# Fixed places for the modulation-weight halves among the product steps, and the gate input's load behind the solve's

## The chip, the cores and the metric

The kernel runs on one core of a Trainium2 chip. The metric is the device time of one execution in microseconds (us), the median of several runs. The engines are PE (TensorE, the matrix multiplier), DVE (VectorE), ACT (ScalarE), POOL (GpSimd) and SP (SyncE, which here issues nearly all DMA transfers). Each engine works through its own instruction list in order and waits for the others by semaphores.

## The reference

The kernel computes one decoder block on x of 512 positions by 1024 columns, all in float32, with a conditioning vector c:

```
mod = silu(c) @ w_ada + b_ada                  # 6 x 1024 numbers
shift1, scale1, gate1, shift2, scale2, gate2 = split(mod, 6)
h = rms_norm(x, norm1_w) * (1 + scale1) + shift1
p = h @ w_in                                   # 47 column tiles of 128
y_a = gated_deltanet(...)                      # recurrence over 8 chunks, gated by silu(z)
y_b = rwkv7_time_mix(...)                      # recurrence over 8 chunks
merged = sigmoid(gl_a) * (y_a @ w_branch_gdn) + sigmoid(gl_b) * (y_b @ w_branch_rwkv)
x = x + gate1 * (merged @ w_out)
h = rms_norm(x, norm2_w) * (1 + scale2) + shift2
x = x + gate2 * conv_glu(h, w_ffn_in, conv_ffn, w_ffn_out)
return rms_norm(x, norm_f_w)
```

What matters here is `mod`: its parts 1 and 2 are needed at the very start, gate1 at the product with w_out, shift2 and scale2 at the second norm (ahead of the first product of the channel mixer), and gate2 at the end.

## The kernel before

Everything is held transposed: 128 columns on the partitions, 512 positions along the row. A weight tile is 128 x 1024. Each weight and each input is split in a high and a low part of type fp32r (`whi`, `wlo`; `hh`, `hl`), and `mm3` makes three matmuls of one product step (lines 186, 189 and 190): high by high, high by low, low by high. A product of eight steps is 24 matmuls. The split of a weight tile is a cast on ACT (`whi<-raw`, L145) and a subtraction on DVE (`wlo<-raw,whi`, L148); there are two buffers each of `raw`, `whi` and `wlo`.

The large products wait in a list, `queue`, and `stream` hands them out step by step. `fill(n)` puts n steps between the instructions of the small, latency-bound stages, `need` goes on until a product is done, and `drain` empties the list. The order of the program is: input norm and the first seven tiles of w_in; the preparation of the gated delta rule with a triangular solve; its recurrence (8 chunks); the preparation of the second solve, `rsolve` (L843 to L849); the gate stage, in which the gated delta output is multiplied with silu(z) and becomes the input of the eight branch products `bg`; the second recurrence (RWKV-7, 8 chunks); the eight branch products `br`, the two last gate tiles among them (`last_gate`); the eight products `o` with w_out, each with its residual on DVE (L1027); the second norm (L307 to L309); the 44 products `fi` and the eight products `fo` of the channel mixer. The products T_RK, T_RR, T_RV, T_Z, T_GA and T_GB are tiles of w_in, in this order from tile 15 to 46.

The modulation weights are worked on DVE, not PE: one column tile j of `mod` is a product and sum along the row of a 128 x 1024 piece of w_ada with `cond`. Tiles 0 to 15 are done ahead of the first product. The other 32 are cut in two halves each, 64 in all, kept in `ada_rest` in order of j. `ada_half` loads one half (256 KB) on SP into the tile `wada`, of which there is one buffer, and reduces it on DVE (L209) with a second short instruction that reads the accumulator. The second half of a tile starts from the sum of the first. `A2` (L1057) is (1 + scale2) * norm2_w for the second norm and needs tiles 32 to 39, that is the first 48 halves of `ada_rest`.

A scheduler takes the program as written and orders each engine's list by data, buffers and its own costs; `tc.add_manual_dep` with `after` adds a constraint on this order only, without a wait on the chip. In the kernel before, `stream` calls `ada_half` for `late` halves when it takes up a product (3 for each T_GA, 4 for six T_GB, 2 for each o), with no constraint except that the first reduce stands behind one instruction of the preparation (`last["gate"]`).

In the gate stage each of four `zt` tiles is loaded from `zsc` (L871), put through Silu on ACT, and multiplied on DVE (L873); `zt` has the two buffers of the tag `sg`. The second solve starts by loading `lt` from `lsc_r` (L563), and DVE scales it (L564).

Of the kernel before, what the change touches and what calls it, by code (L numbers as in the profile page):

```python
# [18 lines left out]
ALU = mybir.AluOpType  # L19
# [4 lines left out]
T = 512  # L24
KT = 8
# [30 lines left out]
def body(ctx, tc, io, out, tap=lambda name, ap: None):  # L56
# [20 lines left out]
    mm = lambda: bank("mm", 2)  # L77
# [97 lines left out]
        pe.matmul(p, ones_r, lo, start=False, stop=True)  # L175


    last = {"step": None, "hold": False, "gate": None, "norm": None}

    def step(*a, **k):  # L180
        last["step"] = pe.matmul(*a, **k)  # L181
# [1 line left out]
    def mm3(p, w, j, x, start, stop):  # L183
        hi, lo = (a[j] for a in w)
        xh, xl = x
        i = pe.matmul(p, hi, xh, start=start, stop=False)  # L186
        if last["hold"]:
            tc.add_manual_dep(i.ins, last["step"].ins.name, after, reason="place")
        pe.matmul(p, hi, xl, start=False, stop=False)  # L189
        pe.matmul(p, lo, xh, start=False, stop=stop)  # L190
        return i


# [8 lines left out]
        if last["norm"] is not None:  # L202
            tc.add_manual_dep(i.ins, last["norm"].ins.name, after, reason="place")

    def ada_half(j, u):
        w = wp.tile([128, T], F32, name="wada", tag="wada")
        part = slice(T * u, T * u + T)
        sp.dma_start(w, io["w_ada"][j][:, part])
        i = dve.tensor_tensor_reduce(out=w, in0=w, in1=cond[:, part], scale=1.0,  # L209
                                 scalar=half[:, j:j + 1] if u else col("b_ada", j), op0=ALU.mult, op1=ALU.add,  # L210
                                 accum_out=(mod if u else half)[:, j:j + 1])
        if last["gate"] is not None:
            tc.add_manual_dep(i.ins, last["gate"].ins.name, after, reason="place")
            last["gate"] = None

    first_half = []
    ada_rest = [(j, u) for j in range(16, 48) for u in range(2)]


# [10 lines left out]
    def stream():  # L230
        while queue:
            it = queue.pop(0)
            for nx in [it] + queue[:it["ahead"]]:
                if nx["begin"] is not None:
                    nx["begin"]()
                    nx["begin"] = None
            for _ in range(min(it["late"], len(ada_rest))):
                ada_half(*ada_rest.pop(0))
            for i, q in enumerate(it["pieces"]):
                for a in (it["pieces"][i:] + [b for nx in queue[:2] for b in nx["pieces"]])[:2]:  # L240
                    if a["w"] is None:
                        a["w"] = weights(a["src"], a["n"] * 128, a["spare"])
                if it["halves"]:
                    continue
                if i == 0:
                    p = it["psum"]()
                for k in range(q["n"]):
                    at = q["k0"] + k
                    mm3(p, q["w"], k, it["xs"][at], at == 0, at == it["n"] - 1)
                    if at == it["n"] - 1:  # L250
                        it["evac"](p)
                        done.add(it["label"])
                    yield
            for u in range(2 if it["halves"] else 0):
                part = slice(H * u, H * u + H)
                p = it["psum"]()[:, 0:H]
                for q in it["pieces"]:
                    for k in range(q["n"]):
                        at = q["k0"] + k
                        mm3(p, q["w"], k, [x[:, part] for x in it["xs"][at]], at == 0, at == it["n"] - 1)  # L260
                        yield
                it["evac"](p, u, part)
                done.add(it["label"])
# [120 lines left out]
    sp.dma_start(cons, io["cons"])  # L384

    def inproj(t, evac, psum=mm, begin=None):
        queue.append(product(t, io["w_in"][t], hx, evac, psum, late=4 if t >= T_GB else 3 if t >= T_GA else 0, begin=begin))


    omu = const.tile([128, 15], F32, name="omu")  # L390
# [93 lines left out]
    dve.tensor_tensor(s3, s3, s1, op=ALU.mult)  # L484
    dve.scalar_tensor_tensor(s3, sx, 0.0, s3, op0=ALU.max, op1=ALU.add)
    fn(nea, col("a_log", 0, 4), AF.Exp)
    last["gate"] = dve.scalar_tensor_tensor(gl, s3, -1.0, bc(nea), op0=ALU.mult, op1=ALU.mult)


    def l2norm(dst, scale):  # L490
# [62 lines left out]
    def solve(sv, name, work):  # L553


        lsc = dr.tile([128, 32, 32], F32, name=f"lsc_{name}")
        tsc = dr.tile([128, 32, 32], F32, name=f"tsc_{name}")
        usc = dr.tile([128, 32, 32], F32, name=f"usc_{name}")
        for e, b, i0, rows in quads():
            sp.dma_start(lsc[i0:i0 + 32].rearrange("i s t -> s i t"), sv[rows, :, 32 * b:32 * b + 32])  # L560
        wk = slot(work).rearrange("p (a t s) -> p a t s", a=2, t=32)
        lt, ti = wk[:, 0], wk[:, 1]
        sp.dma_start(lt, lsc)  # L563
        dve.tensor_scalar(ti, lt.rearrange("p s t -> p t s"), -1.0, None, op0=ALU.mult)  # L564
        pool.affine_select(out=ti, in_=ti, pattern=[[1, 32], [-1, 32]], base=0, channel_multiplier=0,
                           compare_op=ALU.is_gt, fill=0.0)
        pr = tp.tile([128, 1024], F32, name="pr", tag="pr")
        for j in range(1, 31):
            n = 31 - j
            q = pr[:, :n * j].rearrange("p (t c) -> p t c", c=j)  # L570
            dve.tensor_tensor(q, lt[:, j, j + 1:32].unsqueeze(2).broadcast_to([128, n, j]),
                              ti[:, j, 0:j].unsqueeze(1).broadcast_to([128, n, j]), op=ALU.mult)
            dve.tensor_tensor(ti[:, j + 1:32, 0:j], ti[:, j + 1:32, 0:j], q, op=ALU.subtract)
        dve.memset(ti.rearrange("p t s -> p (t s)")[:, ::33], 1.0)
        sp.dma_start(tsc, ti)
        tt = pr.rearrange("p (s t) -> p s t", s=32)
        act.copy(tt, ti.rearrange("p t s -> p s t"))
        sp.dma_start(usc, tt)
        t1 = lt
        for e, b, i0, rows in quads():  # L580
            if b == 1:
                pool.memset(sv[rows, :, 0:32], 0.0)
            sp.dma_start(sv[rows, :, 32 * b:32 * b + 32], usc[i0:i0 + 32].rearrange("i s t -> s i t"))
            if b == 0:
                sp.dma_start(t1[rows], tsc[i0:i0 + 32].rearrange("i t s -> t i s"))
        yield
        for h in range(2):
            i_ = slice(16 * h, 16 * h + 16)
            p = pa().rearrange("p (i t) -> p i t", i=16)
            ht = tmp("sg").rearrange("p (i t) -> p i t", i=16)  # L590
            for i in range(16):
                for e in range(2):
                    lo_r, hi_r = slice(64 * e, 64 * e + 32), slice(64 * e + 32, 64 * e + 64)
                    pe.matmul(p[hi_r, i, :], sv[lo_r, 16 * h + i, 32:64], t1[lo_r, 16 * h + i, :],
                              start=True, stop=True)
            fill(2)
            for e in range(2):
                hi_r = slice(64 * e + 32, 64 * e + 64)
                act.copy(ht[hi_r], p[hi_r])
            p = pa().rearrange("p (i t) -> p i t", i=16)  # L600
            for i in range(16):
                for e in range(2):
                    lo_r, hi_r = slice(64 * e, 64 * e + 32), slice(64 * e + 32, 64 * e + 64)
                    pe.matmul(p[lo_r, i, :], ht[hi_r, i, :], sv[hi_r, 16 * h + i, 32:64],
                              start=True, stop=True)
            fill(2)
            for e in range(2):
                lo_r = slice(64 * e, 64 * e + 32)
                act.mul(sv[lo_r, i_, 32:64], p[lo_r], -1.0)
# [258 lines left out]
    ga_l = [tmp_r(tag) for tag in ("acc", "acc", "sq", "sq")]  # L868
    for ct in range(4):
        zt, sg = tmp("sg"), tmp("rs")  # L870
        sp.dma_start(zt, zsc[ct])  # L871
        fn(zt, zt, AF.Silu)
        dve.tensor_tensor(sg, go[:, ct], zt, op=ALU.mult)  # L873
        split(ga_h[ct], ga_l[ct], sg)
# [137 lines left out]
    for n in range(KT):  # L1012
        if n in (0, 3):
            g = KT - 2 + n // 3
            queue.append(product(T_GB + g, io["w_in"][T_GB + g], hx, last_gate(g), ahead=1))
        queue.append(product(("br", n), io["w_br"][n], bx, merge(n), begin=merge_in(n), ahead=1))
    x2s = [slot(9), slot(3)]
    x2 = lambda k: x2s[k // 4][:, T * (k % 4):T * (k % 4) + T]
    for n in range(KT):
# [29 lines left out]
        rstd_of(p, 1.0 / D, rstd2[:, part])  # L1049

    for n in range(KT):
        queue.append(product(("o", n), io["w_out"][n], mx, residual(n, x2, 16, keep, total2), late=2, halves=n == KT - 1))
    need(("o", KT - 2))
    table(EXP)
    while ada_rest:
        ada_half(*ada_rest.pop(0))
    dve.scalar_tensor_tensor(A2, mod[:, 32:40], 1.0, col("norm2", 0, 8), op0=ALU.add, op1=ALU.mult)  # L1057
    rstd2 = tmp("rs")
    drain()
# [43 lines left out]
        return f  # L1103

    for i in range(7, 2 * NF):
        queue.append(product(("fi", i), io["w_fi"][i], h2, (glu_up if i % 2 else glu_gate)(i // 2)))
    prefetch()
    for i in range(7):
        (glu_up if i % 2 else glu_gate)(i // 2)(ffn_ps[i])
# [114 lines left out]
```

## Time and profile before

| what | value |
| --- | --- |
| median of 3 runs | 935.42 us (933.39 to 936.28) |
| the profiled execution | 937.31 us, span 935.6 us |
| PE busy | 876.3 us (94%) |
| DVE busy | 533.3 us (57%) |
| ACT busy | 419.2 us (45%) |
| halves of the modulation weights | 64 loads from 47.2 to 476.5 us of the span, 2.7 us from issue to landing (median) |

The span is the time from the first to the last instruction that the profiler saw. Busy time is the sum over an engine's instructions. In the rows that follow, "L186 PE MATMUL ps_mm<-hh,whi" is an instruction of line 186 on PE that writes `ps_mm` and reads `hh` and `whi`; "[4.70 <-ACT tmp_sp L94]" says that the engine was idle for 4.70 us before it and that an instruction of line 94 on ACT, which writes `tmp_sp`, ended that wait. PEld is PE's loading of weights, which overlaps its matmuls. PEclk is the granted clock of PE as a share of full speed.

### The profile page before, as it was taken

The numbers are of one execution on the slowest core, as the hardware profiler recorded it, in microseconds if no ns is written. First come the engines' busy times: TensorE is split into PE (matmuls) and PEld (weight loads), VectorE is DVE, ScalarE is ACT, GpSimd is POOL, SyncE is SP. The second block draws the span as 40 slices with busy tenths as digits, with TensorE's granted clock in tenths as the row PEclk, the third lists the DMA queues.
The fourth block names the chain that finished last, engine by engine and source line by source line (L and its number), as shares of the span: only waits on it lengthen the run. The fifth ranks groups of instructions, "written<-read, shape, count | busy, mean of one in ns | idle before, by whom it ended". The sixth has DMA issues, their size and how long they took to land.

```text
span 935.6 us, 13853 instructions
## 1 busy us (share of the span) xinstructions
PE 876.3 (94%) x5459; PEld 687.7 (74%) x5459; DVE 533.3 (57%) x858; ACT 419.2 (45%) x680; POOL 95.2 (10%) x91
## 2 busy tenths in 40 slices
PE   2999999999989978899999999999999999999996
PEld 1886577677656666677668888888888888888885
DVE  5987859824696786255476537564445445332233
ACT  5367543734554747632465335343333333333231
POOL 1000300000352300001230120000000000010112
PEclk9999999997999989899999999999999999999998
DMA  9841245363323367644546542322322322533322
GB/s 332 283 149 67 91 105 185 109 166 112 103 82 113 69 213 267 162 147 148 183 158 202 171 141 84 111 91 92 109 92 90 105 99 90 179 98 100 107 80 91
DMA packets 81119, 125.72 MB, mean 134 GB/s; under 512 B 26045, under 2 KB 42813, under 8 KB 80990
## 3 DMA queue, kind: packets, MB, share of 16 engines
q1 hardware_dynamic: 81054, 124.83, 42.2%
q8 instruction: 43, 0.70, 0.3%
q14 instruction: 22, 0.18, 0.1%
HBM read 110.13 MB, written 14.16 MB: 133 GB/s over the span
## 4 chain that ended last, share of the span: by engine, by line
PE 69%; DVE 10%; DMA 6%; ACT 6%; issue 6%; POOL 2%; SPq 0%; DVEq 0%; POOLq 0%; ACTq 0%
PE ps_mm L186 19%; PE ps_mm L189 18%; PE ps_mm L190 18%; DMA wada<-in_w_ada 4%; DVE wlo L148 2%; PE ps_pc L181 2%; DVE wada L209 1%; ACT tmp_rs L94 1%; PE ps_pc L186 1%; PE ps_pc L189 1%; PE ps_pc L190 1%; ACT slot L619 1%; PE ps_pa L186 1%; PE ps_pa L189 1%; PE ps_pa L190 1%
## 5 line engine op out<-in xcount | busy, mean ns | idle before, releaser
L186 PE MATMUL ps_mm<-hh,whi 128*128 128x512 f32 (+1 forms) x642 | 264.2, 412 | 9.8 <-ACT hh L308 3.4
L148 DVE TENSOR_TENSOR wlo<-raw,whi 128x1024 fp32r<-128x1024 f32 (+2 forms) x140 | 161.2, 1152 | 176.2 <-ACT whi L145 170.6
L190 PE MATMUL ps_mm<-hh,wlo 128*128 128x512 f32 (+1 forms) x642 | 255.0, 399 | 1.3 <-DVE wlo L148 1.3
L189 PE MATMUL ps_mm<-hl,whi 128*128 128x512 f32 (+1 forms) x642 | 253.8, 396 | 0.0
L145 ACT CAST whi<-raw 128x1024 fp32r<-128x1024 f32 (+2 forms) x140 | 137.1, 979 | 259.7 <-PE ps_mm L189 198.4
L186 PEld LDWEIGHTS ps_mm<-hh,whi 128*128 128x128 f32 x642 | 121.5, 190 | 46.8 <-issue 8.5
L190 PEld LDWEIGHTS ps_mm<-hh,wlo 128*128 128x128 f32 x642 | 121.6, 189 | 31.6 <-issue 3.4
L189 PEld LDWEIGHTS ps_mm<-hl,whi 128*128 128x128 f32 x642 | 122.1, 190 | 26.7 <-issue 4.0
L186 PE MATMUL ps_mm<-slot,whi 128*128 128x512 f32 (+1 forms) x226 | 85.7, 379 | 4.7 <-ACT tmp_sp L94 4.7
L190 PE MATMUL ps_mm<-slot,wlo 128*128 128x512 f32 (+1 forms) x226 | 85.1, 376 | 0.0
L189 PE MATMUL ps_mm<-slotd,whi 128*128 128x512 f32 (+1 forms) x168 | 62.4, 371 | 0.0
L186 PEld LDWEIGHTS ps_mm<-slot,whi 128*128 128x128 f32 x226 | 43.2, 191 | 12.6 <-ACT tmp_sp L94 4.9
L190 PEld LDWEIGHTS ps_mm<-slot,wlo 128*128 128x128 f32 x226 | 43.1, 191 | 7.7
L189 PE MATMUL ps_mm<-slot,whi 128*128 128x512 f32 (+1 forms) x122 | 45.3, 372 | 0.0
L186 PE MATMUL ps_mm<-slotd,whi 128*128 128x512 f32 (+1 forms) x96 | 36.4, 379 | 0.0
L190 PE MATMUL ps_mm<-slotd,wlo 128*128 128x512 f32 (+1 forms) x96 | 36.1, 376 | 0.0
L209 DVE CUSTOM_DVE_ANT_0 wada<-wada,cond,cols 128x512 f32<-128x512 f32 x32 | 25.6, 800 | 18.3 <-DMA wada<-in_w_ada 18.2
L189 PEld LDWEIGHTS ps_mm<-slotd,whi 128*128 128x128 f32 x168 | 31.6, 188 | 5.7
L1099 DVE TENSOR_TENSOR tmp_sg<-tmp_acc,ps_mm 128x512 f32<-128x512 f32 x20 | 13.8, 688 | 36.0 <-PE ps_mm L190 35.8
L209 DVE CUSTOM_DVE_ANT_0 wada<-wada,cond,half 128x512 f32<-128x512 f32 x32 | 24.9, 779 | 14.6 <-DMA wada<-in_w_ada 14.4
L398 DVE SCALAR_TENSOR_TENSOR tmp_acc<-ps_mm,cols,tmp_acc 128x511 f32<-128x511 f32 (+2 forms) x44 | 32.8, 746 | 0.7
L1032 POOL COPY tmp_rs<-tmp_sq 128x512 f32<-128x512 f32 x2 | 2.1, 1064 | 304.0 <-ACT tmp_sq L1029 304.0
(270 smaller groups left out, 1262.5 us busy)
## 6 DMA issues: line engine op xcount, KB each, us to landing
raw<-in_w_in SPq DMA_DIRECT2D x40, 512.0 KB, 4.1
raw<-in_w_fi SPq DMA_DIRECT2D x37, 512.0 KB, 3.5
wada<-in_w_ada SPq DMA_DIRECT2D x64, 256.0 KB, 2.7
raw<-in_w_fo SPq DMA_DIRECT2D x16, 512.0 KB, 3.6
slot<-in_w_ada SPq DMA_DIRECT2D x10, 512.0 KB, 8.5
slot<-in_xT SPq DMA_DIRECT2D x16, 256.0 KB, 4.6
raw<-in_w_out SPq DMA_DIRECT2D x8, 512.0 KB, 3.4
raw<-in_w_in SPq DMA_DIRECT2D x8, 448.0 KB, 4.5
```

The costliest lines, as they stand in the source:

```text
L94: i = act.activation(*a, **k)
L145: i = act.copy(hi, src)
L148: j = eng.tensor_tensor(lo, src, hi.bitcast(F32), op=ALU.subtract)
L181: last["step"] = pe.matmul(*a, **k)
L186: i = pe.matmul(p, hi, xh, start=start, stop=False)
L189: pe.matmul(p, hi, xl, start=False, stop=False)
L190: pe.matmul(p, lo, xh, start=False, stop=stop)
L209: i = dve.tensor_tensor_reduce(out=w, in0=w, in1=cond[:, part], scale=1.0, scalar=half[:, j:j + 1] if u else col("b_ada", j), op0=ALU.mult ...
L398: dve.scalar_tensor_tensor(acc[:, i:], p[:, :T - i], w[:, taps - 1 - i:taps - i], acc[:, i:], op0=ALU.mult, op1=ALU.add)
L619: (act.copy if e == c or quiet else dve.tensor_copy)(place(e, 2 * b + c), p[hs(c), :, e, :])
L1032: pool.tensor_copy(sums[0], sq)
L1099: dve.tensor_tensor(t, accs[j], p, op=ALU.mult)
```

## The change

Each half is now split in a load (`ada_load`) and a reduce (`ada_half`), and both are constrained in order to a step of the product in hand: the load behind the last matmul so far at the step with `at % gap == 0`, the reduce behind that of step `gap - 1` or 4. `late` is handed out anew: one half for each of the eight T_RK and T_RR products, two for each T_GB and each last gate, one for each br, three, three and two for the o products (none for the last), and one for each of 16 fi products. The loop that took the remaining halves ahead of A2 is gone. Apart from that, the loads of `zt` are constrained to stand behind the solve's load of `lt`. The core of the diff:

```diff
-    def ada_half(j, u):
+    def at_step(i):
+        if last["mm"] is not None:
+            tc.add_manual_dep(i.ins, last["mm"].ins.name, after, reason="place")
+
+    def ada_load(j, u):
         w = wp.tile([128, T], F32, name="wada", tag="wada")
-        part = slice(T * u, T * u + T)
-        sp.dma_start(w, io["w_ada"][j][:, part])
-        i = dve.tensor_tensor_reduce(out=w, in0=w, in1=cond[:, part], scale=1.0,
-                                 scalar=half[:, j:j + 1] if u else col("b_ada", j), op0=ALU.mult, op1=ALU.add,
-                                 accum_out=(mod if u else half)[:, j:j + 1])
-        if last["gate"] is not None:
-            tc.add_manual_dep(i.ins, last["gate"].ins.name, after, reason="place")
-            last["gate"] = None
+        at_step(sp.dma_start(w, io["w_ada"][j][:, T * u:T * u + T]))
+        return j, u, w
+
+    def ada_half(j, u, w):
+        at_step(dve.tensor_tensor_reduce(out=w, in0=w, in1=cond[:, T * u:T * u + T], scale=1.0,
+                                         scalar=half[:, j:j + 1] if u else col("b_ada", j), op0=ALU.mult, op1=ALU.add,
+                                         accum_out=(mod if u else half)[:, j:j + 1]))
...
-            for _ in range(min(it["late"], len(ada_rest))):
-                ada_half(*ada_rest.pop(0))
+            todo, loaded = min(it["late"], len(ada_rest)), None
+            gap = it["n"] // todo if todo else 0
...
+                    if todo and at % gap == 0 and at // gap < todo:
+                        loaded = ada_load(*ada_rest.pop(0))
                     mm3(p, q["w"], k, it["xs"][at], at == 0, at == it["n"] - 1)
+                    if loaded and at % gap == min(gap - 1, 4):
+                        ada_half(*loaded)
+                        loaded = None
...
-        queue.append(product(t, io["w_in"][t], hx, evac, psum, late=4 if t >= T_GB else 3 if t >= T_GA else 0, begin=begin))
+        queue.append(product(t, io["w_in"][t], hx, evac, psum, late=2 if t >= T_GB else 1 if T_RK <= t < T_RV else 0,
+                             begin=begin))
...
-        sp.dma_start(lt, lsc)
+        last["load"] = sp.dma_start(lt, lsc)
...
-        sp.dma_start(zt, zsc[ct])
+        i = sp.dma_start(zt, zsc[ct])
+        tc.add_manual_dep(i.ins, last["load"].ins.name, after, reason="place")
...
-            queue.append(product(T_GB + g, io["w_in"][T_GB + g], hx, last_gate(g), ahead=1))
-        queue.append(product(("br", n), io["w_br"][n], bx, merge(n), begin=merge_in(n), ahead=1))
+            queue.append(product(T_GB + g, io["w_in"][T_GB + g], hx, last_gate(g), late=2, ahead=1))
+        queue.append(product(("br", n), io["w_br"][n], bx, merge(n), late=1, begin=merge_in(n), ahead=1))
...
-        queue.append(product(("o", n), io["w_out"][n], mx, residual(n, x2, 16, keep, total2), late=2, halves=n == KT - 1))
+        queue.append(product(("o", n), io["w_out"][n], mx, residual(n, x2, 16, keep, total2),
+                             late=3 if n < 2 else 2 if n < KT - 1 else 0, halves=n == KT - 1))
...
-    while ada_rest:
-        ada_half(*ada_rest.pop(0))
...
-        queue.append(product(("fi", i), io["w_fi"][i], h2, (glu_up if i % 2 else glu_gate)(i // 2)))
+        queue.append(product(("fi", i), io["w_fi"][i], h2, (glu_up if i % 2 else glu_gate)(i // 2), late=1))
```

The lines of the kernel after are some nine higher: L209 is L216 there, L307 is L315, L1027 is L1037, L1057 is L1066, L871 is L880 and L563 is L572.

DVE's list at the end of the o products, before (L1027 is a residual, the last two of half a row each; L307 and L309 are the second norm, which reads `A`, that is A2):

```order
L1027 SCALAR_TENSOR_TENSOR slot_4387<-ps_mm,mod,slot_4387 128x512
L148 TENSOR_TENSOR wlo<-raw,whi 128x896
L1027 SCALAR_TENSOR_TENSOR slot_4387<-ps_mm,mod,slot_4387 128x256
L307 SCALAR_TENSOR_TENSOR tmp_acc<-slot_4386,A_103,tmp_rs 128x256
L309 SCALAR_TENSOR_TENSOR hl_5079<-tmp_acc,mod,hh_5071 128x256
L1027 SCALAR_TENSOR_TENSOR slot_4387<-ps_mm,mod,slot_4387 128x256
L148 TENSOR_TENSOR wlo<-raw,whi 128x896
```

The same place after, from the last residual on, with the numbers of the buffers (each L216 pair is a reduce and its accumulator read):

```order
L1037 SCALAR_TENSOR_TENSOR slot3_4303<-ps_mm_4989,mod_100,slot3_4303 128x256
L216 ISA wada_4791,half_101<-wada_4791,cond_79,cols_77 128x512
L216 ISA half_101 128x1
L148 TENSOR_TENSOR wlo_5115<-raw_5048,whi_5114 128x896
L216 ISA wada_4806,mod_100<-wada_4806,cond_79,half_101 128x512
L216 ISA mod_100 128x1
```

These are the first two of the eight; on the same list, behind the four more pairs, come the last two, A2 (L1066) and the norm (L315):

```order
L216 ISA wada_4917,half_101<-wada_4917,cond_79,cols_77 128x512
L216 ISA half_101 128x1
L216 ISA wada_4932,mod_100<-wada_4932,cond_79,half_101 128x512
L216 ISA mod_100 128x1
L1066 SCALAR_TENSOR_TENSOR A2_103<-mod_100,cols_77 128x8
L315 SCALAR_TENSOR_TENSOR tmp_acc_5050<-slot9_4302,A2_103,tmp_rs_4954 128x256
```

Before, A2 stands in the second recurrence and the norm follows the first half of the last residual; after, eight halves stand between the last residual and A2, and the whole norm stands behind them.

SP's list at the same place, before and then after (`raw<-in_w_fi` of 128x7x128 are the weights of the first seven fi tiles, `xsc` keeps the residual):

```order
L319 DMA raw<-in_w_fi 128x7x128
L1046 DMA xsc<-slot_4387 128x512
L319 DMA raw<-in_w_fi 128x7x128
L1046 DMA xsc<-slot_4387 128x256 x2
L319 DMA raw<-in_w_fi 128x7x128 x5
```

```order
L1056 DMA xsc<-slot_4303 128x256
L212 DMA wada<-in_w_ada 128x512
L327 DMA raw<-in_w_fi 128x7x128
L212 DMA wada<-in_w_ada 128x512 x6
L327 DMA raw<-in_w_fi 128x7x128 x4
```

Seven loads of halves have moved behind the last `xsc`, six of them in a row.

ACT's list at the gate stage, before and then after (`tmp_sg<-tmp_sg` is Silu on a `zt` tile, `tmp_sp<-ps_mm` empties the accumulator that PE fills next, `slot<-tmp_rs` casts bg's input):

```order
L88 ACT_TABLE_LOAD
L94 ACTIVATE tmp_sg<-tmp_sg 128x512 x2
L145 CAST whi<-raw 128x512
L145 CAST slot_2753<-tmp_rs 128x512 x2
L94 ACTIVATE tmp_sg<-tmp_sg 128x512 x2
L88 ACT_TABLE_LOAD
L145 CAST slot_2753<-tmp_rs 128x512 x2
L94 ACTIVATE tmp_sp<-ps_mm 128x512 x2
```

```order
L88 ACT_TABLE_LOAD
L145 CAST whi<-raw 128x512 x2
L94 ACTIVATE tmp_sg<-tmp_sg 128x512 x2
L145 CAST slot_2768<-tmp_rs 128x512 x2
L94 ACTIVATE tmp_sg<-tmp_sg 128x512 x2
L145 CAST slot_2768<-tmp_rs 128x512
L88 ACT_TABLE_LOAD
L145 CAST slot_2768<-tmp_rs 128x512
L94 ACTIVATE tmp_sp<-ps_mm 128x512 x2
```

The casts of the first two bg weight tiles have moved ahead of the first Silu, and one cast ahead of the second table load. On SP, all four loads of `zt` now follow the load of `lt`:

```order
L569 DMA lsc_r<-slotd_2487 32x32x32 x4
L705 DMA asc<-tmp_sp 128x512
L156 DMA raw<-in_w_bg 128x512 x2
L572 DMA slot_2691<-lsc_r 128x1024
L880 DMA tmp_sg<-zsc 128x512 x2
L156 DMA raw<-in_w_bg 128x512
L880 DMA tmp_sg<-zsc 128x512 x2
```

Before, the first two `zt` loads stood nine and six rows ahead of the four `lsc_r` transfers, the other two directly ahead of `lt`, and `lt` ahead of the two weight loads.

More of the change, by code (lines that the diff above doesn't have):

```diff
@@ L175, in block_sum @@
         pe.matmul(p, ones_r, lo, start=False, stop=True)
-    last = {"step": None, "hold": False, "gate": None, "norm": None}
+    last = {"mm": None, "step": None, "hold": False, "norm": None}
     def step(*a, **k):
@@ L189, in mm3 @@
         pe.matmul(p, hi, xl, start=False, stop=False)
-        pe.matmul(p, lo, xh, start=False, stop=stop)
+        last["mm"] = pe.matmul(p, lo, xh, start=False, stop=stop)
         return i
@@ L203, in ada @@
             tc.add_manual_dep(i.ins, last["norm"].ins.name, after, reason="place")
-    def ada_half(j, u):
+    def at_step(i):
+        if last["mm"] is not None:
+            tc.add_manual_dep(i.ins, last["mm"].ins.name, after, reason="place")
+    def ada_load(j, u):
         w = wp.tile([128, T], F32, name="wada", tag="wada")
-        part = slice(T * u, T * u + T)
-        sp.dma_start(w, io["w_ada"][j][:, part])
-        i = dve.tensor_tensor_reduce(out=w, in0=w, in1=cond[:, part], scale=1.0,
-                                 scalar=half[:, j:j + 1] if u else col("b_ada", j), op0=ALU.mult, op1=ALU.add,
-                                 accum_out=(mod if u else half)[:, j:j + 1])
-        if last["gate"] is not None:
-            tc.add_manual_dep(i.ins, last["gate"].ins.name, after, reason="place")
-            last["gate"] = None
-    first_half = []
+        at_step(sp.dma_start(w, io["w_ada"][j][:, T * u:T * u + T]))
[4 more added lines that the diff above has]
+                                         accum_out=(mod if u else half)[:, j:j + 1]))
     ada_rest = [(j, u) for j in range(16, 48) for u in range(2)]
@@ L486, in body @@
     fn(nea, col("a_log", 0, 4), AF.Exp)
-    last["gate"] = dve.scalar_tensor_tensor(gl, s3, -1.0, bc(nea), op0=ALU.mult, op1=ALU.mult)
+    dve.scalar_tensor_tensor(gl, s3, -1.0, bc(nea), op0=ALU.mult, op1=ALU.mult)
     def l2norm(dst, scale):
```

## The prediction

> **What bounds the kernel now.** I read the page first, then the chain, then the group of modulation loads, then the waits of PE stage by stage.
>
> ```profile
> span 935.6 us, 13853 instructions
> PE 876.3 (94%) x5459; PEld 687.7 (74%) x5459; DVE 533.3 (57%) x858; ACT 419.2 (45%) x680; POOL 95.2 (10%) x91
> by line: PE ps_mm L186 18.8%; PE ps_mm L189 18.3%; PE ps_mm L190 18.3%; issue 5.8%; DMA wada<-in_w_ada 4.4%; DVE wlo L148 2.1%; PE ps_pc L181 2.0%; DVE wada L209 1.4%; ACT tmp_rs L94 1.4%; PE ps_pc L186 1.2%; PE ps_pc L189 1.1%; PE ps_pc L1
>   DMA wada<-in_w_ada: 32.5, 25
> ```
>
> PE is busy for 876.3 of 935.6 us, so all its idle time is 59 us. The chain puts 4.4 + 1.4 = 5.8% (54 us) on the modulation halves (`wada`), and DVE sat idle 32.5 us for their loads, yet little of that reaches PE. The waits of PE in four windows (88 to 125, 125 to 210, 210 to 300 and 395 to 457 us; columns: total, times, longest), those that DVE ends:
>
> ```profile
> PE ps_pa L635 <- DVE slotd L639: 1.1, 1, 1.1
> PE ps_pa L518 <- DVE tmp_acc L514: 1.1, 1, 1.1
> PE ps_mm L186 <- DVE slot L398: 1.5, 1, 1.5
> PE ps_mm L190 <- DVE wlo L148: 1.3, 2, 0.8
> PE ps_pa L760 <- DVE tmp_sq L756: 1.9, 3, 0.7
> PE ps_pc L181 <- DVE ck L793: 1.6, 2, 1.3
> PE ps_pc L181 <- DVE cz L785: 1.2, 2, 0.7
> PE ps_pc L181 <- DVE slotd L907: 0.6, 1, 0.6
> ```
>
> They sum to 10.3 us. One half costs, by the timeline (start, duration, engine):
>
> ```profile
> 297.11 0.75 DVE L209 CUSTOM_DVE_ANT_0 wada<-wada,cond,cols 128x512 f32<-128x512 f32 x1 [0.50 <-DMA wada<-in_w_ada]
> 297.78 0.08 DVE L209 DVE_READ_ACCUMULATOR2_ANT half<- 128x1 f32 x1
> 297.89 3.81 SPq L208 DMA_DIRECT2D wada<-in_w_ada  x2
> 300.58 0.75 DVE L209 CUSTOM_DVE_ANT_0 wada<-wada,cond,half 128x512 f32<-128x512 f32 x1 [2.72 <-DMA wada<-in_w_ada]
> ```
>
> There is one `wada` buffer, so the next load leaves only after the reduce before it: 0.83 us of DVE, but 300.58 - 297.11 = 3.47 us from reduce to reduce when nothing else is due. That cycle decides the forecast.
>
> **Term 1, the halves leave the early stages: -11 us.** The gated delta solve, its recurrence, the preparation of the second solve and that solve hold no half any more; eight stand in the RK stage. Of the 10.3 us I take 8, because L907 and part of the L148 and L398 waits remain. In the L848 stage a load is itself on the chain:
>
> ```profile
> 305.47 2.58 DMA wada<-in_w_ada
> 308.97 2.96 DMA wada<-in_w_ada
> ```
>
> The pieces behind these loads are short copies with PE partly fed, so I count about half of 5.54 us, 3. Bounds: -5 (the 1.1 to 1.9 us waits come from DVE's own work, not from halves) to -17 (all 10.3 + 5.5, and 1 for SP's shorter queue).
>
> **Term 2, the gate input behind the solve's load: +6 us.** The timeline at the gate stage:
>
> ```profile
> 325.31 1.15 ACT L94 ACTIVATE tmp_sg<-tmp_sg 128x512 f32<-128x512 f32 x2
> 326.37 0.60 ACT L145 CAST whi<-raw 128x512 fp32r<-128x512 f32 x1
> 326.69 1.99 SPq L871 DMA_DIRECT2D tmp_sg<-zsc  x2
> 329.92 0.63 ACT L94 ACTIVATE tmp_sg<-tmp_sg 128x512 f32<-128x512 f32 x1 [1.90 <-DMA tmp_sg<-zsc]
> 330.58 0.69 DVE L873 TENSOR_TENSOR tmp_rs<-slotd,tmp_sg 128x512 f32<-128x512 f32 x1 [1.51 <-ACT tmp_sg L94]
> 331.75 1.28 ACT L88 ACT_TABLE_LOAD   x1
> 334.74 0.79 PE L186 MATMUL ps_mm<-slot,whi 128*128 128x512 f32 x1 [4.70 <-ACT tmp_sp L94]
> ```
>
> Two `sg` buffers hold four `zt` tiles. Before, the first two were loaded long ahead, so one round trip is exposed: load to Silu to multiply, 326.69 to 331.27 = 4.6 us. Now all four loads follow `lt` on SP, and `lt` follows two weight loads of bg, the second of which waits for `wlo` of bg0. So the first pair goes out near 327.3, its multiplies end near 332.5, and the second pair goes out only then, when its buffers are free: a second round trip. DVE's solve scaling and the cast of bg1 now also stand ahead of the first multiply. Last multiply near 337.5, table load 1.28, cast and evacuation near 340.6: PE restarts 6 us after 334.74. What else waits is little: the solve's load leaves some 2 us earlier, and its steps lie beside bg's products. Bounds: -2 (`lt` first helps the solve, the first pair is early anyway) to +10 (two whole round trips).
>
> **Term 3, ten halves in the br stage: +4.5 us.** The windows (us, then busy us of PE, PEld, DVE, ACT, POOL, PEclk, DMA share, GB/s):
>
> ```profile
> 330.00:334.70 4.70, 0.03 (x1) 0.00 (x0) 3.33 (x4) 4.11 (x7) 1.16 (x1) 0.85 0.85 309
> 334.70:340.10 5.40, 5.37 (x13) 4.20 (x14) 5.09 (x17) 1.20 (x3) 0.10 (x1) 0.50 0.54 194
> 490.00:522.00 32.00, 32.00 (x143) 26.50 (x142) 23.54 (x35) 16.20 (x24) 0.00 (x0) 1.00 0.62 193
> 522.00:562.00 40.00, 39.74 (x197) 33.71 (x197) 14.67 (x16) 12.96 (x18) 10.86 (x7) 1.00 0.44 148
> 590.00:610.00 20.00, 20.00 (x90) 16.53 (x89) 12.09 (x16) 9.28 (x13) 0.00 (x0) 1.00 0.33 105
> ```
>
> DVE is busy 23.54 of 32 us there; ten halves add 8.3, which makes 31.8. An in-order engine at 99% with loads, casts and PE to wait for runs over; bounds 0 and +8.3, the middle taken. The o stage has room: 14.67 of 40, plus ten halves of 0.83.
>
> **Term 4, A2 behind eight halves: +30 us.** On DVE eight halves and their accumulator reads now stand between the last residual and A2, and the norm needs A2. Before, A2 was ready since the second recurrence:
>
> ```profile
> 561.27 0.48 DVE L307 SCALAR_TENSOR_TENSOR tmp_acc<-slot,A,tmp_rs 128x256 f32<-128x256 f32 x1 [2.57 <-ACT tmp_rs L94]
> 562.50 0.47 PE L186 MATMUL ps_mm<-hh,whi 128*128 128x256 f32 x1
> 562.74 0.48 DVE L1027 SCALAR_TENSOR_TENSOR slot<-ps_mm,mod,slot 128x256 f32<-128x256 f32 x1
> ```
>
> In these clock times: the last residual ends at 563.22; the first half follows at once (its load is in flight), the eighth starts 7 x 3.47 = 24.3 later, at 587.5, and ends at 588.4; A2 about 0.2; norm to first matmul 562.50 - 561.27 = 1.2: 589.8 to 590.0, against 562.50, +27.5. No other PE work is left to fill it: the seven fi tiles all read `hh`. Then PE comes back at half clock. After the 4.70 us idle the granted clock was 0.50 for 5.40 us and 13 matmuls; at the dense rate, 20/90 = 0.222 us each, they need 2.9, so 2.5 is lost. 27.5 + 2.5 = 30. Bounds: seven cycles of 3.3 us and no half clock, 26; of 3.9 and the half clock, 34.
>
> The Trainium skill, "TensorE: Matmul & The Clock Gate", Part 1, says that the array runs at half rate until it has been busy for one window of about 3.4 us; by it the loss would be 1.7 us and the sum 0.8 lower, an estimate from that page. The row of 5.40 us at 0.50 decides for the longer time here.
>
> **Term 5, the other places: 0.** Twelve halves stay with the T_GB products in and behind the second recurrence, where DVE cost PE only the 0.6 us of L907; they hide there as before. Sixteen go to the fi products: one of eight steps takes 24 x 0.222 = 5.3 us against one half's 3.47, and DVE is busy 12.09 of 20; that slack is the cover. Without it each late half would cost up to 0.83; bounds 0 to +3.
>
> Sum: -11 + 6 + 4.5 + 30 + 0 = +29.5. The profiled execution took 937.31 us (1.7 around its span), 1.9 above the median of 935.42; against the median the sum gives 965.
>
> **Rivals.**
> A. The A2 wait alone: bg is covered and DVE holds the br stage. -11 + 30 = +19, 954. For it: br's PE is at 32.00 of 32.00, so nothing was late there. Against it: the table load and two round trips stand in ACT's order.
> B. The stall's cycle is slower. Loads share the queue and the engines with fi's weights; this load took 4.13:
>
> ```profile
> 235.35 4.13 DMA wada<-in_w_ada
> ```
>
> Seven cycles of 4.13 + 0.83 = 34.7 instead of 24.3: +10, 975. Against it: six loads stand in a row on SP with no weight load between.
> C. The stall doesn't come because the halves run ahead and A2 is early: -11 + 6 = -5, 930. It asks that the eight reduces leave DVE before the last residual; DVE's order has them behind it, so only a reading error of mine gives this.
> D. Faster, by the chain: the 54 us of loads and reduces come off the end while terms 2 to 4 stay: -54 + 40.5 = -13.5, 922. It decides from 40.5 us of gain on; PE's waits on DVE sum to a quarter of that.
>
> **Chances.** Forecast 0.66 (957 to 972), A 0.17, B 0.10, C 0.04, D 0.03. A and B bound the range; with the ends of terms 1 and 3 it runs from 948 to 978. Changes within 0.3% (2.8 us) can't be told from none. C ends 0.6% faster, with a small part within: faster 0.06, same 0.02, slower 0.92.
>
> **What would show it.** A PE gap of about 27 us ahead of the first fi matmul, released in the end by `hh`, with DVE's reduces 3.5 us apart in it; a granted clock of half behind it; a gap ahead of bg's first product of about 10 us instead of 4.70; PE's DVE waits before 300 us down to 2 or 3 us. I am wrong if the reduces in the gap are nearer than 3 us or fewer than eight, or if fi's halves open gaps in its 5.3 us products.

## The result, and the profile after

The kernel after takes 984.93 us (median of 4 runs, 984.81 to 988.61) against 935.85 (933.39 to 938.29): slower by 5.4%, ratio 1.0541 with a 95% interval of 1.0524 to 1.0558. That is 49 us where 29.5 were forecast, beyond the upper end of the range. The page of the kernel after, its first lines:

```profile
span 983.3 us, 13858 instructions
PE 885.0 (90%) x5459; PEld 694.6 (71%) x5459; DVE 532.8 (54%) x858; ACT 418.9 (43%) x680; POOL 91.9 (9%) x91
```

DVE and ACT are busy as long as before (533.3 and 419.2 us), and PE 9 us longer; the other 39 us of PE are idle time. The longer busy time goes with a lower clock: the mean granted clock is 0.954 against 0.983 before, and a large part of the difference lies in the second solve (0.67 from 366 to 388 us, against 0.90 from 365 to 400 before). The waits of PE by window say where (300 to 340, 457 to 510, 510 to 580 and 580 to 640 us; columns: total, times, longest):

```profile
PE ps_mm L186 <- ACT tmp_sp L94: 12.3, 1, 12.3
PE ps_mm L186 <- ACT whi L145: 2.7, 1, 2.7
PE ps_mm L190 <- DVE wlo L148: 2.8, 4, 1.2
PE ps_pa L1048 <- ACT tmp_sq L1039: 2.3, 1, 2.3
PE ps_pa L1047 <- POOL tmp_rs L1044: 1.0, 1, 1.0
PE ps_mm L186 <- ACT hh L316: 26.1, 1, 26.1
```

The first is the gap ahead of the first product of bg, 4.7 us before. The next four lie in the br and o stages, where PE waited for almost nothing before. The last is the gap ahead of the first fi product. DVE in that gap, and PE behind it (timeline: start, duration; four reduces left out):

```profile
581.49 0.48 DVE L1037 SCALAR_TENSOR_TENSOR slot<-ps_mm,mod,slot 128x256 f32<-128x256 f32 x1 [3.44 <-PE ps_mm L190]
582.00 0.75 DVE L216 CUSTOM_DVE_ANT_0 wada<-wada,cond,cols 128x512 f32<-128x512 f32 x1
...
585.59 0.75 DVE L216 CUSTOM_DVE_ANT_0 wada<-wada,cond,half 128x512 f32<-128x512 f32 x1 [1.82 <-DMA wada<-in_w_ada]
...
603.82 0.75 DVE L216 CUSTOM_DVE_ANT_0 wada<-wada,cond,cols 128x512 f32<-128x512 f32 x1 [2.94 <-DMA wada<-in_w_ada]
...
607.31 0.75 DVE L216 CUSTOM_DVE_ANT_0 wada<-wada,cond,half 128x512 f32<-128x512 f32 x1 [2.74 <-DMA wada<-in_w_ada]
...
608.11 0.17 DVE L1066 SCALAR_TENSOR_TENSOR A<-mod,cols 128x8 f32<-128x8 f32 x1
608.31 0.88 DVE L315 SCALAR_TENSOR_TENSOR tmp_acc<-slot,A,tmp_rs 128x256 f32<-128x256 f32 x2
```

```profile
609.39 0.79 PE L186 MATMUL ps_mm<-hh,whi 128*128 128x256 f32 x2 [26.11 <-ACT hh L316]
```

Eight reduces from 582.00 to 607.31, seven intervals of 3.62 us on the mean. The first finds its load landed, the second waits 1.82 us after a `wlo`, and the other six wait near 3 us each for their own loads: the stall is as forecast. What was missed lies elsewhere.

The gate stage after, SP and ACT (timeline):

```profile
320.70 0.33 SPq L572 DMA_DIRECT2D slot<-lsc_r  x1
321.08 1.86 SPq L880 DMA_DIRECT2D tmp_sg<-zsc  x2
328.08 1.26 SPq L880 DMA_DIRECT2D tmp_sg<-zsc  x2
```

```profile
325.71 1.33 ACT L94 ACTIVATE tmp_sg<-tmp_sg 128x512 f32<-128x512 f32 x2 [2.97 <-DMA tmp_sg<-zsc]
330.87 0.63 ACT L94 ACTIVATE tmp_sg<-tmp_sg 128x512 f32<-128x512 f32 x1 [1.22 <-DMA tmp_sg<-zsc]
333.44 1.28 ACT L88 ACT_TABLE_LOAD   x1
335.26 1.08 ACT L94 ACTIVATE tmp_sp<-ps_mm 128x512 f32<-128x512 f32 x2
```

and on DVE the first multiply:

```profile
326.38 1.68 DVE L883 TENSOR_TENSOR tmp_rs<-slotd,tmp_sg 128x512 f32<-128x512 f32 x1 [0.24 <-ACT tmp_sg L94]
```

The two round trips are there: the first pair of loads, issued at 321.08, reaches Silu at 325.71 (4.6 us), its first multiply ends at 328.06, and the second pair leaves at 328.08, when that buffer is free.

### The profile page after: what moved, and what is told of

It is laid out like the page before. It is cut to its first block, busy times and chain, and to the rows that moved or that the text cites. A ratio compares the mean times of both kernels' runs of the same rounds, so it can differ in the third digit from the quotient of the medians.

```text
span 983.3 us, 13858 instructions
## 1 busy us (share of the span) xinstructions
PE 885.0 (90%) x5459; PEld 694.6 (71%) x5459; DVE 532.8 (54%) x858; ACT 418.9 (43%) x680; POOL 91.9 (9%) x91
## 4 chain that ended last, share of the span: by engine, by line
PE 66%; ACT 9%; DVE 9%; DMA 9%; issue 4%; POOL 1%; SPq 0%; DVEq 0%; ACTq 0%; POOLq 0%
PE ps_mm L186 18%; PE ps_mm L190 17%; PE ps_mm L189 17%; DMA wada<-in_w_ada 6%; PE ps_pc L181 3%; ACT slot L628 2%; DVE wlo L148 2%; ACT tmp_rs L94 2%; DVE wada L216 1%; ACT whi L145 1%; PE ps_pc L186 1%; PE ps_pc L190 1%; PE ps_pc L189 1%; PE ps_pa L186 1%; PE ps_pa L190 1%
## 5 line engine op out<-in xcount | busy, mean ns | idle before, releaser
L186 PE MATMUL ps_mm<-slot,whi 128*128 128x512 f32 (+1 forms) x226 | 86.3, 383 | 12.4 <-ACT tmp_sp L94 12.3
L216 DVE CUSTOM_DVE_ANT_0 wada<-wada,cond,cols 128x512 f32<-128x512 f32 x32 | 25.0, 782 | 26.6 <-DMA wada<-in_w_ada 26.4
L216 DVE CUSTOM_DVE_ANT_0 wada<-wada,cond,half 128x512 f32<-128x512 f32 x32 | 26.9, 840 | 22.6 <-DMA wada<-in_w_ada 22.5
L94 ACT ACTIVATE tmp_acc<-tmp_acc 128x512 f32<-128x512 f32 x22 | 13.9, 633 | 41.6 <-DVE tmp_acc L407 41.5
```

The lines of the kernel that those rows point to most:

```text
L94: i = act.activation(*a, **k)
L216: at_step(dve.tensor_tensor_reduce(out=w, in0=w, in1=cond[:, T * u:T * u + T], scale=1.0, scalar=half[:, j:j + 1] if u else col("b_ada", j ...
```

## The experiments

Medians, all against the runs of the kernel before on the same chip (934.88 to 935.36 us):

| run | what it is | us | ratio, 95% interval |
| --- | --- | --- | --- |
| e4_before_nohalves | before, no halves at all | 935.78 | 1.0004 (0.9991 to 1.0016) |
| e1_before_dep | before + constraint on zt | 944.69 | 1.0110 (1.0086 to 1.0134) |
| e10_no_places | after, ties to steps removed | 943.92 | 1.0091 (1.0071 to 1.0111) |
| e5_after_nohalves | after, no halves at all | 942.40 | 1.0084 (1.0064 to 1.0104) |
| e2_after_nodep | after, no constraint on zt | 975.82 | 1.0441 (1.0413 to 1.0469) |
| e3_own_buffers | after, own buffers ahead of A2 | 959.08 | 1.0252 (1.0224 to 1.0280) |
| e11_no_br | e3, br's halves left out | 949.68 | 1.0146 (1.0131 to 1.0161) |
| e12_no_br_no_dep | e11, no constraint on zt | 939.02 | 1.0042 (1.0026 to 1.0058) |
| e14_no_br_no_o | after, no constraint, br's and o's halves left out | 935.79 | 1.0014 (1.0000 to 1.0027) |
| e7_br_only | after, no constraint, eight halves from o to T_GA | 947.48 | 1.0131 (1.0111 to 1.0151) |
| e8_even | after, no constraint, none in br, halves in every product | 941.12 | 1.0065 (1.0046 to 1.0084) |
| e13_zt_sp | before, two more buffers for zt | 939.61 | 1.0038 (1.0025 to 1.0051) |

**What were the halves worth before?** e4_before_nohalves leaves all of them out:

```diff
-    ada_rest = [(j, u) for j in range(16, 48) for u in range(2)]
+    ada_rest = []
+    dve.memset(mod[:, 16:48], 0.0)
```

> The kernel before with all 64 halves left out; their columns of the modulation are set to zero. This is the most that any placement can give. Theory T (the halves were nearly hidden before, since DVE's own work makes PE's early waits): 930 to 933 us, and PE's waits on DVE before 300 us still sum to 7 us or more. Rival R (they cost the 11 us that the prediction took, and the kernel after lost them elsewhere again): 920 to 925 us, and PE's waits on DVE before 300 us fall to 2 or 3 us. The chain's shares read as time to be had: 882 us.

935.78 us against 934.97: nothing, less even than the 2 to 5 us of theory T. PE's waits for DVE in it, in the same early windows (88 to 125, 125 to 210, 210 to 300 us):

```profile
PE ps_pa L636 <- DVE slotd L640: 0.7, 1, 0.7
PE ps_pa L519 <- DVE tmp_acc L515: 0.2, 1, 0.2
PE ps_mm L186 <- DVE slot L399: 1.7, 1, 1.7
PE ps_mm L190 <- DVE wlo L148: 1.1, 2, 0.5
PE ps_pa L761 <- DVE tmp_sq L757: 1.8, 3, 0.7
PE ps_pc L181 <- DVE cz L786: 0.7, 1, 0.7
```

6.2 us of the 9.7 that these windows had before stay with no half on DVE: those waits belong to DVE's other work. The other 3.5 do go (PE ends the gate preparation, L861, at 316.49 instead of 320.62), and then come back as waits on other work: the gap ahead of bg is 5.1 instead of 4.7, and in the windows from 335 to 400 us PE waits for the second solve's copies on ACT and for `wlo`. At 393 us the lead is 1.8, and the span ends 1.1 us shorter. So Rival R and the reading of the chain (54 us to be had) both fall: even with the halves gone the interval leaves at most 1 us, so a better place for them had next to nothing to give. One reservation holds for this run and all that follow: the scheduler orders each version anew, so a difference of a few us between two runs can hold a change of order besides the one that is named.

**The constraint on zt.** e1_before_dep adds it to the kernel before, e2_after_nodep takes it from the kernel after; e5_after_nohalves is the kernel after with no halves, by the edit of e4.

```diff
-        sp.dma_start(lt, lsc)
+        last["load"] = sp.dma_start(lt, lsc)
...
-        sp.dma_start(zt, zsc[ct])
+        i = sp.dma_start(zt, zsc[ct])
+        tc.add_manual_dep(i.ins, last["load"].ins.name, after, reason="place")
```

> The kernel before with one edit: the loads of zt stand behind the load of lt. Theory T (the gate stage's loss is this constraint alone, a second round trip of two zt loads ahead of the cast of bg's input): the idle time of PE ahead of bg's first product grows from 4.7 to 11 to 13 us, the run takes 944 to 947 us. Rival G (the gap comes from the halves' new places and the constraint costs nothing): 936 us, gap 4.7.

> The kernel after without the constraint on the zt loads; the halves stay at their new places. Theory T: 974 to 977 us, the gap ahead of bg's first product back at 4 to 5 us. Rival G: 985 us, gap 12 us.

> The kernel after with all 64 halves left out; their columns of the modulation are set to zero; the constraint on the zt loads stays. Theory T: the run without halves of the kernel before plus 8 to 10 us, 939 to 943 us; no gap ahead of the first fi product and none in the br stage. Rival G: the same as the kernel before without halves.

944.69, 975.82 and 942.40 us, all within the ranges of theory T. The constraint costs 9.7 us in the kernel before, 9.1 in the kernel after, and 6.6 where there are no halves at all (942.40 - 935.78), less than the 8 to 10 that theory T added there. The wait ahead of bg's first product, in e1, e2 and e5 in this order:

```profile
PE ps_mm L186 <- ACT tmp_sp L94: 12.6, 1, 12.6
PE ps_mm L186 <- ACT tmp_sp L94: 5.1, 1, 5.1
PE ps_mm L186 <- ACT tmp_sp L94: 12.7, 1, 12.7
```

The gap follows the constraint and not the halves; Rival G falls. That the two buffers of `zt` make the second round trip is read from the rows of the kernel after: the second pair leaves at 328.08, when the first multiply has ended (328.06). No run has the constraint with four buffers, so this step is not tested by itself.

**The places.** e10_no_places keeps the counts and the constraint on zt, and drops the ties to steps (`at_step` does nothing).

> The kernel after without the constraints that tie loads and reduces to steps; counts per product and the constraint on the zt loads stay. The scheduler then puts all 64 halves early, as before. Theory T: the run is the kernel before plus the gate stage: 943 to 947 us. If the counts and not the ties make the stalls: 965 us or more.

943.92 us: the scheduler puts the halves early again (their loads run from 45.9 to 464.3 us) and what is left is the constraint on zt. All the rest of the loss is made by the ties.

**The wait ahead of A2.** e3_own_buffers gives the last halves ahead of A2 tiles of their own, in two slots that are free after br:

```diff
-        w = wp.tile([128, T], F32, name="wada", tag="wada")
+        w = own.pop(0) if own and len(ada_rest) < 24 else wp.tile([128, T], F32, name="wada", tag="wada")
...
+    own = []
...
+    need(("br", KT - 1))
+    own.extend(quarter(slot(2)) + quarter(slot(12)))
```

> The kernel after with one edit: the last seven or eight halves ahead of A2 are loaded into tiles of their own that are free by then, so that their loads needn't wait for the reduce before; counts and places of the halves stay the same. Theory T (the stall ahead of the first fi product is the cycle of load and reduce through one buffer, and not DVE's work): the gap of 26 us goes, and what is left are the gate stage's 9 and the br stage's 8: 951 to 957 us. Rival W (the reduces themselves, tied to late steps, hold A2 up): a gap of 7 us or more stays, 960 us or more. Rival Q (the loads share queue and engines with the first fi weights, so the wait only moves to those): over 965 us.

959.08 us, 25.9 below the kernel after, 2 us over theory T's end. PE ahead of and at the first fi product:

```profile
PE ps_pa L1048 <- POOL tmp_rs L1045: 2.3, 1, 2.3
PE ps_mm L186 <- ACT hh L317: 0.4, 1, 0.4
```

The same number of reduces costs nothing there once the loads needn't queue for one buffer: 26.1 became 0.4. The order changed with it: in e3's list on DVE all eight stand ahead of the last half of the last residual, and A2 starts at 576.80 us, with that residual at 581.86. Rivals W and Q fall.

**The br and o stages.** From e3 on, e11_no_br leaves the eight halves of br out, e12_no_br_no_dep drops the constraint on zt as well, and e14_no_br_no_o is the kernel after (one buffer) without the constraint and with the halves of br and o left out (`in ("br", "o")` in the edit).

```diff
-                        loaded = ada_load(*ada_rest.pop(0))
+                        jj, uu = ada_rest.pop(0)
+                        if isinstance(it["label"], tuple) and it["label"][0] == "br":
+                            dve.memset((mod if uu else half)[:, jj:jj + 1], 0.0)
+                        else:
+                            loaded = ada_load(jj, uu)
```

> The kernel with own buffers for the last halves (e3_own_buffers), and the eight halves of the br products left out (their sums set to zero). Theory T: the br stage's loss goes and the gate stage's stays: 944 to 948 us, PE in the br stage without waits for casts and wlo. Rival C (the br stage's loss is not from its halves): 957 us or more.

> The same, and without the constraint on the zt loads; the halves of the T_RK, T_RR, T_GB and o products and of fi stand at the fixed places of the kernel after. Theory T: all of the loss is accounted for: 934 to 938 us. If the fixed places cost something of their own there: 940 us or more.

> The kernel after without the constraint on the zt loads, and with the 24 halves of the br and o products left out (their sums set to zero). Left at fixed places are 8 in T_RK and T_RR, 16 in T_GB and the last gates, 16 in fi. Theory T (what the run without br halves and without the constraint still lost, some 4 us, is lost in the o products, where wlo stands behind reduces that wait for their loads): 934 to 937 us, no PE wait for wlo in the o stage. Rival (fixed places cost something wherever they are, fi included): 939 us or more.

949.68, 939.02 and 935.79 us. The eight halves of br cost 9.4 (959.08 - 949.68; e11 is some 2 us above its expected end, as e3 was), the constraint 10.7 (949.68 - 939.02), and the rest, 3.7 over the 935.3 of before, is lost in the main in the o products (e14 leaves 0.9 of it).

The traces show both stages longer. The first merge of br and the first residual of o on DVE, before and then after:

```profile
492.79 0.69 DVE L992 TENSOR_TENSOR tmp_acc<-tmp_sq,ps_mm 128x512 f32<-128x512 f32 x1 [1.60 <-PE ps_mm L190]
522.71 0.75 DVE L1027 SCALAR_TENSOR_TENSOR slot<-ps_mm,mod,slot 128x512 f32<-128x512 f32 x1 [1.48 <-PE ps_mm L190]
```

```profile
498.17 0.68 DVE L1002 TENSOR_TENSOR tmp_acc<-tmp_sq,ps_mm 128x512 f32<-128x512 f32 x1
535.71 0.75 DVE L1037 SCALAR_TENSOR_TENSOR slot<-ps_mm,mod,slot 128x512 f32<-128x512 f32 x1 [0.82 <-PE ps_mm L190]
```

From the one to the other it is 29.9 us before, 37.5 in the kernel after, and 30.4 in e11. From there to the last residual it is 40.0 us before (562.74), 45.8 after (581.49), 44.4 in e12 and 40.0 in e14; it is 40.0 in e8 too, which has none in br and eight halves in o in place of 16. DVE in both stages of the kernel after (490 to 575 us), and the way to PE's longest wait in br:

```profile
DVE wada L216 <- DMA wada<-in_w_ada: 20.8, 13, 3.3
497.49 0.75 DVE L216 CUSTOM_DVE_ANT_0 wada<-wada,cond,half 128x512 f32<-128x512 f32 x1 [1.36 <-DMA wada<-in_w_ada]
499.48 0.33 SPq L156 DMA_DIRECT2D raw<-in_w_br  x1
504.07 0.62 ACT L145 CAST whi<-raw 128x512 fp32r<-128x512 f32 x1 [2.29 <-DMA raw<-in_w_br]
504.79 0.47 PE L186 MATMUL ps_mm<-hh,whi 128*128 128x512 f32 x1 [2.70 <-ACT whi L145]
```

The reduce at 497.49 waited for its load. The merge and a `wlo` (498.76, 0.68 us) stood behind it on DVE, and the next weight load left at 499.48, when that `wlo` had ended. So a late half on DVE also makes weight loads late. The loads were slower in themselves as well: 4.2 us from issue to landing (median of the weight loads, 490 to 535 us) against 3.4 before (490 to 522). How the cost of br divides between the two was not tested.

PE's waits in the o products of e12 (window 510 to 575 us) first, then DVE's (515 to 560 us):

```profile
PE ps_mm L190 <- DVE wlo L148: 2.6, 3, 1.4
PE ps_pa L1051 <- POOL tmp_rs L1048: 1.4, 1, 1.4
```

```profile
DVE wada L216 <- DMA wada<-in_w_ada: 10.1, 7, 2.8
```

DVE sat seven times, 10.1 us, at the head of its list waiting for a half to land, with `wlo` and residuals behind. With the o halves gone as well (e14) these waits are gone, and the time is that of before. So the 16 halves in T_GB and the last gates, the 8 in T_RK and T_RR and the 16 in fi cost little if anything: 0.9 us, with an interval from nothing to 2.5.

**Versions that might have been faster.** e7_br_only moves eight halves from o to T_GA; e8_even has halves in every product from T_RK on and none in br; e13_zt_sp gives zt two more buffers in the kernel before.

```diff
-        late=2 if t >= T_GB else 1 if T_RK <= t < T_RV else 0
+        late=2 if t >= T_GB else 1 if T_RK <= t < T_RV or t >= T_GA else 0     # e7
+        late=2 if t >= T_GB else 1 if t >= T_RK else 0                         # e8
...
-        queue.append(product(("br", n), io["w_br"][n], bx, merge(n), late=1, begin=merge_in(n), ahead=1))
+        queue.append(product(("br", n), io["w_br"][n], bx, merge(n), begin=merge_in(n), ahead=1))    # e8
...
-        late=3 if n < 2 else 2 if n < KT - 1 else 0
+        late=2 if n == 0 else 1 if n < KT - 1 else 0                           # e7, e8 (o products)
...
-        zt, sg = tmp("sg"), tmp("rs")
+        zt, sg = tmp("sg" if ct < 2 else "sp"), tmp("rs")                      # e13
```

> The kernel after without the constraint on the zt loads, and with eight of the halves of the o products handed to the eight T_GA products, so that A2 stands ahead of the last residual. The ten halves of the br stage stay. Theory T: what is left over the kernel before is the br stage alone, 8 us: 942 to 946 us, with the gaps of PE in the br stage (casts and wlo late) as in the kernel after. Rival C (the br stage lost its 8 us to the late gate stage ahead of it, or to the stall behind it): 935 to 937 us.

> The kernel after without the constraint on the zt loads and without halves in the br products: one half for each product from T_RK to T_GA, two for each T_GB and last gate, eight in the o products, sixteen in fi, all at fixed steps. Theory T: all costs are gone and there is nothing to gain, as in the run without halves: 934 to 938 us. If fixed places away from the early stages are worth something in themselves: 925 to 930 us.

> The kernel before with one edit: the third and fourth zt tile take the two buffers of the tag sp in place of those of sg, so that they needn't wait for the multiplies of the first two. Theory T (round trips of zt set the gap ahead of bg's first product): the gap of 4.7 us shrinks to 1 to 3 us, 930 to 934 us. Rival (the buffers of sp come free no earlier, or ACT's table loads set the gap): 935 us, gap 4 to 5 us.

947.48, 941.12 and 939.61 us: all three above what theory T gave. Against e8, the br halves of e7 cost 6.4 us, less than the 9.4 above. e8 itself stays 6 us over the kernel before, with the gap ahead of bg at 6.1 instead of 4.7; where its other 4 us go is open. e13 shortened that gap to 3.7 us and still came out slower: in its trace PE's place in the program was 1.5 us ahead at L861, level at the last bg product and 2 us behind at the end of the second solve. So a shorter gap is not by itself time to be had; why the second solve took longer there is open.

## Why the prediction was wrong

- Sum. Along one chain of runs the parts are 25.9 (A2), 9.4 (br), 10.7 (zt) and 3.7 (the rest, o in the main). As steps of one chain they add to the 49.6 over the 935.3 of before by construction, so two other ways were taken. e2 less e14 gives 40.0 for A2, br and o together, where the chain gives 39.0. In the two traces the kernel after lags by 5.4 us at the first merge of br, 13.0 at the first residual of o, 18.8 at the last one and 46.9 at the first fi product: 5.4 up to br, 7.6 in br, 5.8 in o and 28.1 ahead of fi. The forecast had -5 up to br (-11 + 6), 4.5 in br, 0 in o and 30.
- Term 1 (-11, bounds -5 to -17): the step that failed most. It took PE's waits that DVE ends for waits that the halves cause. With no half at all the time is the same; nothing in the rows excluded zero, and the bounds should have reached it. The sign that it named failed too: PE's waits for DVE ahead of 300 us were to fall to 2 or 3 us, and they are 6.3 in the kernel after (the same three windows) and 6.2 with no halves. Waits of PE ended by DVE say which engine came last, not what on it was to spare. The lead that e4's trace has at the end of the gate preparation (4.1 us) is down to 1.8 behind the second solve.
- Term 2 (+6, bounds -2 to +10): right in mechanism, undersized. The gap grew by 12.3 - 4.7 = 7.6 us, and taking the constraint away gives 6.6 to 10.7. A round trip, from the issue of a pair's loads to the end of its first multiply, was priced at 4.6 us. The first pair's took 7.0 (321.08 to 328.06): 4.6 to Silu, which took 3.2 before, and 1.68 for a multiply that took 0.69 before. The clock times of the term were off: the first pair left at 321.08 and not near 327.3, PE reached the gap 6.4 us earlier than before, and it restarted at 335.90 and not near 340.6.
- Term 3 (+4.5 for br, the o stage free): undersized, 9.4 by the chain of runs (7.6 in the trace) and 3.7 (5.8 in the trace). The step that failed is the price of a reduce as 0.83 us of DVE's busy time. A reduce at the head of an in-order list costs until its load lands, here up to 3.3 us of waiting, and what stands behind waits with it. For the same reason "14.67 of 40 us busy" was no cover for the o halves.
- Term 4 (+30): right in place and nearly in size. From the start of the last residual to the first fi matmul it is 27.9 us (581.49 to 609.39) where it was -0.2 before (562.74 to 562.50): 28.1 later against the 27.5 worked out, with 3.62 us between reduces against the 3.47 taken; taking it away (e3) gave 25.9. The 2.5 us for the half clock did not show as lag: the kernel after is 46.9 us behind at the first fi matmul (609.39 against 562.50) and 46.8 at the first product of gate and up (649.64 against 602.89). PE did run at half clock behind the gap, for 3.0 us, but without a wait (busy 6.50 of 6.50 us); in the kernel before PE lost time in the same place in other ways, 0.42 us of it in a wait for `hh`. That the two came out level is not something the term foresaw.
- Term 5 (0): right, by e14.
- Rivals. A took the costs of bg and br as covered; both were dearer than forecast. B's slower cycle was 3.62, not 4.96. C asked that the eight reduces leave DVE ahead of the last residual; they stood behind it. D's 54 us of the chain were worth nothing.

## What to carry to other kernels

Before a wait is priced, run the kernel once with the suspected work left out: that bounds the gain, and here it was nothing that could be told although the chain and the waits named the work. In an in-order list an instruction that waits for a load costs the wait of all that stands behind it, so a place for it is safe only where its load has a buffer and has landed; its busy time and the engine's busy share say nothing of that. Where work is tied to late steps, count deadline against cycle: here the 26 halves of br, the second last gate and o had to pass through one buffer at 3.47 us each, 90 us, while these stages lasted 72 (490 to 562 us of the span before). In e7 it was 18 halves, 62 us, and PE waited 0.4 us ahead of the first fi product instead of 26.1.

## What was not expected of the hardware

How long the half clock lasts behind a gap did not follow the gap: 5.4 us behind the 4.70 of before, and less behind the longer gaps after. The windows (us, busy us of PE, PEld, DVE, ACT, POOL, PEclk, DMA share, GB/s) over the gap of 12.28 us and behind it, then the same for that of 26.11 us:

```profile
323.50:335.80 12.30, 0.13 (x2) 0.00 (x0) 9.70 (x22) 6.61 (x11) 1.26 (x1) 0.59 0.36 111
335.80:342.00 6.20, 6.09 (x20) 4.87 (x21) 5.75 (x16) 1.64 (x4) 0.00 (x0) 0.71 0.23 85
583.00:609.50 26.50, 0.39 (x3) 0.11 (x1) 7.26 (x19) 1.56 (x4) 0.00 (x0) 0.54 0.30 90
609.50:616.00 6.50, 6.50 (x43) 6.48 (x44) 6.09 (x12) 3.99 (x7) 0.00 (x0) 0.77 0.00 0
```

If the clock is half or full, a mean of 0.71 over 6.20 us is 3.6 us at half, and 0.77 over 6.50 is 3.0. The idle time ahead counts as well: 0.59 over 12.30 us is 10.1 at half, 0.54 over 26.50 is 24.4, and before, 0.85 over 4.70 us is 1.4 ahead of the 5.4. Each stretch at half, from its start in the gap, is then 6.8, 13.7 and 27.4 us. One more in the trace of before, in the window from 200 to 230 us (0.83), is 10.2. All four are whole multiples of 3.4 us (2, 4, 8 and 3). So in these traces what is left of the half clock behind a gap depends on where the gap ends on that grid, and not on how long it was. The Trainium skill, "TensorE: Matmul & The Clock Gate", Part 1, gives a window of about 3.4 us that runs freely; the traces of before and after agree with it, by these four stretches.
